# RWKV preparation without Pool: paired low-rank halves and attention keys loaded in quarters in an encoder block on one core

## The chip, the core and the metric

The kernel runs on one core of a Trainium2 chip. A core has five engines that run side by side, each working through its own queue in order: PE (matrix products; PEld is its weight load), DVE (vector operations), ACT (scalar functions, with a table of functions that is loaded when another set is needed), POOL (a general vector engine) and SP, which here only issues DMAs. POOL and ACT issue DMAs too. PE writes into PSUM, DVE and ACT read PSUM; POOL reads the on-chip memory SBUF only. Semaphores order the engines among each other. The metric is device time in microseconds (us) from the start to the end of one execution; lower is better.

## The reference

One layer of a bidirectional encoder: one input projection feeds windowed attention, a two-directional RWKV-7 scan and sigmoid gates; then output projection, MLP and a gated input embedding. Sequence 1024, width 1024, 8 RWKV heads of 64. What the changed stage prepares is the RWKV part:

```python
h = rms_norm(x, norm_mix[i])
proj = h @ w_in[i]
...
zr = proj[..., O_RWKV:O_GATE]
zr = zr + shift_mu[i] * (centred_shift(zr) - zr)      # 0.5 * (previous + next token)
...
w_raw = w0 + einsum('btr,drc->dbtc', tanh(wl), w2)    # wl, al: 64 columns of zr each
decay = exp(-exp(-softplus(-w_raw) - 0.5))
a = sigmoid(a0 + einsum('btr,drc->dbtc', al, a2))
kk = k * k_k
kk = kk / maximum(sqrt(sum(kk * kk, axis=-1)), 1e-12)
k_dir = k * (1.0 + (a - 1.0) * k_a)
ys = rwkv7_bidir_scan(r, decay, k_dir, v, -kk, kk * a)
...
bonus = einsum('bthn,dbthn,dhn->bth', r, k_dir, r_k) * v
...
gates = sigmoid(proj[..., O_GATE:])
```

## The kernel before

Activations stand with channels on the 128 rows and tokens along the columns. A product in float32 is made of three matmuls on rounded parts: `split` (L186) rounds a tile to its high part on ACT and subtracts it for the low part on DVE, or on the engine given as `lo_eng`. `load_w` brings a 1024 x 128 block of weights in two DMAs of 256 KB, each with a `split` whose low half is POOL's unless it says otherwise. A projection of 128 channels is 2 halves of 512 tokens x 8 blocks x 3 = 48 matmuls (`proj_steps`, `proj_with`).

The preparation goes over four pairs of heads p. For each pair:

- `keys(p)` projects and mixes the key (`shifted`, L532), squares it into `nrm[:, 0]` (L644) and splits the square; `sums2` (L593, L594) sums it over each head's channels on PE.
- `normed_keys` projects the receptance r; behind its 38th matmul (RH = 36) the sums are put on PE and clamped by DVE (L655). ACT then takes logarithm and exponential (L658, L659, a table load each), DVE makes kk (L661).
- `direction(d, p, ...)` for d = 0, then, after the value projection, for d = 1. `lora` makes two low-rank products (i = 0 the decay `th`, i = 1 the in-context rate `ta`): per half of the tokens a product over all 128 rows (L569) that carries high x high and low x high together, and one over 64 rows (L571). Two full ones, two half-row ones, then the same for the other i. Then scaling on ACT (L670), a running sum on DVE (`TENSOR_TENSOR_SCAN`, L672, with the constant `scan`), E and Ei = exp of plus and minus the sum on ACT (L682, L683), the operands ra and bk (L687, L688 on POOL, L695, L696), kd (L691, L692) and rk for the bonus (L698 to L701). ra and bk go to DRAM.
- `add_bonus` of a pair runs during the next pair: rk split and summed on PE, the value turned by PE transposes (L607), product bv on DVE (L612).

`shifted` copies the projection to zr on ACT (L539) and writes it scaled by 1 - mu (L542); POOL adds the two neighbours (sm, L544), DVE multiplies by mu/2 and adds (L545).

In the last pair, `fill0` draws steps from `gates0`, the sigmoid gates' projection of the first token half (24 matmuls a gate; F0 tells how many steps where). What is left of `gates0` runs at low priority among the attention's matmuls. After pair 2, one POOL DMA of 2 MB loads the attention's keys kT (L727) into the room of `nrm` (tag `yk`). Attention starts with the queries' DMA, also on POOL (L879), and its scores `sc` (L894).

What order the instructions of an engine take is decided by a scheduler from the order of the code, priorities and dependencies; an operation may be pinned with `keep_in_program_order` (`mmo` is a pinned matmul). Tiles of one tag share `bufs` buffers, and a new tile waits until the old one in its buffer is done with.

Of the kernel before, what the change touches and what calls it, by code (L numbers as in the profile page):

```python
# [9 lines left out]
F32 = mybir.dt.float32  # L10
F32R = mybir.dt.float32r
# [30 lines left out]
RH = 36  # L42
# [11 lines left out]
F0 = (28, 28, 28, 28, 40)  # L54
# [84 lines left out]
def block_kernel(ctx: ExitStack, tc: tile.TileContext, I: dict, out: bass.AP):  # L139
# [45 lines left out]

    def split(hi, lo, src, lo_eng=None, pin=False):  # L186

        a = nc.scalar.copy(hi, src)  # L188
        b = (lo_eng or nc.vector).tensor_tensor(out=lo, in0=src, in1=hi.bitcast(F32), op=ALU.subtract)  # L189
        if pin:  # L190
            tc.keep_in_program_order(a)
            tc.keep_in_program_order(b)
# [111 lines left out]
    def gates(h, ms=range(2 * KT), mm=nc.tensor.matmul):  # L304

        for m in ms:
            c0 = O_GATE + m * P
            hi, lo = load_w(PW, "w", w_in[:, :, c0:c0 + P], P, parts=2)
# [189 lines left out]
    with ExitStack() as s1:  # L498
# [15 lines left out]
        nc.vector.memset(wsc, W_SCALE)  # L514
        hka = A1.tile([P, 4], F32, name="hka")
# [7 lines left out]
        for i in range(2):  # L523
            st = A1.tile([P, ND, 512], F32, name="wlrst", tag="th", bufs=2)
# [4 lines left out]
        scan = A1.tile([P, T], F32, name="scan")  # L529
        nc.sync.dma_start(scan, I["scan"])  # L530

        def shifted(c0, mi, pss=None, pin=False):  # L532
            pss = pss or proj(c0)
            zr = A1.tile([P, T + 2], F32, name="zr", bufs=1)
            nc.vector.memset(zr[:, 0:1], 0.0)
            nc.vector.memset(zr[:, T + 1:T + 2], 0.0)
            zc = z = A1.tile([P, T], F32, name="z", bufs=4)
            for h in range(2):
                a = nc.scalar.copy(zr[:, 1 + 512 * h:513 + 512 * h], pss[h])  # L539
                if pin and h == 0:  # L540
                    tc.keep_in_program_order(a)
                nc.scalar.activation(out=zc[:, 512 * h:512 * h + 512], in_=pss[h], func=AF.Copy, scale=omm[:, mi:mi + 1])  # L542
            sm = A1.tile([P, T], F32, name="sm", bufs=1)
            nc.gpsimd.tensor_tensor(out=sm, in0=zr[:, 0:T], in1=zr[:, 2:T + 2], op=ALU.add)  # L544
            a = nc.vector.scalar_tensor_tensor(out=z, in0=sm, scalar=hmu[:, mi:mi + 1], in1=zc, op0=ALU.mult, op1=ALU.add)  # L545
            if pin:
                tc.keep_in_program_order(a)
# [10 lines left out]
        sg = A1.tile([P, T], F32, name="sg", tag="th", bufs=2)  # L558
# [4 lines left out]
        def lora(d, p, i, bias_col):  # L563

            th = A1.tile([P, T], F32, name="th", bufs=2)
            cs_, hss = slice(p * P, (p + 1) * P), [slice(512 * h, 512 * h + 512) for h in range(2)]
            pss = [PX.tile([P, 512], F32, name="px", tag="px", bufs=6) for _ in range(2)]
            for ps, hs in zip(pss, hss):
                nc.tensor.matmul(ps, wlr_h[i][:, d, cs_], lr[i][:, hs], start=True, stop=False)  # L569
            for ps, hs in zip(pss, hss):  # L570
                nc.tensor.matmul(ps, wlr_l[hrows[i], d, cs_], lr[i][hrows[i], hs], start=False, stop=True)  # L571
            for h, ps in enumerate(pss):
                nc.scalar.activation(out=th[:, 512 * h:512 * h + 512], in_=ps, func=AF.Tanh, scale=0.5, bias=hb[:, bias_col:bias_col + 1])
            return th
# [41 lines left out]
        gates0 = gates(0)  # L616
# [21 lines left out]

        nrm = PY.tile([P, 2, T], F32, name="nrm", tag="yk")

# [8 lines left out]
        def normed_keys(p, kz, sums):  # L649

            ri = nrm[:, 1]

            def norms():
                for hs, ps in next(sums):
                    nc.vector.tensor_scalar_max(ri[:, hs], ps, 1e-24)  # L655
# [6 lines left out]
            return kz, rz, kk  # L662
# [3 lines left out]

# [1218 lines left out]
```

## Time and profile before

| | us |
|---|---|
| three runs, median | 3303.46 |
| lowest and highest of the three | 1796.93, 4185.17 |
| the profiled execution's own time | 1788.35 |
| its span, first to last instruction | 1786.6 |
| preparation, first key matmul to first score | 122.8 to 369.7 |
| mean granted PE clock | 0.98 |

A profile row of the timeline gives start and duration in us, engine, line, operation, output <- inputs, shapes and how often (x); in brackets stands how long the engine was idle before it and what ended that. A row of the waits gives who waited for whom, total us, times, longest. A row of windows gives, for a stretch, its length and each engine's busy us and instructions (x). A row of DMA issues ends with KB each and us from issue to landing.

### The profile page before, as it was taken

The numbers are of one execution on the slowest core, as the hardware profiler recorded it, in microseconds if no ns is written. First come the engines' busy times: TensorE is split into PE (matmuls) and PEld (weight loads), VectorE is DVE, ScalarE is ACT, GpSimd is POOL, SyncE is SP. The second block draws the span as 40 slices with busy tenths as digits, with TensorE's granted clock in tenths as the row PEclk, the third lists the DMA queues.
The fourth block names the chain that finished last, engine by engine and source line by source line (L and its number), as shares of the span: only waits on it lengthen the run. The fifth ranks groups of instructions, "written<-read, shape, count | busy, mean of one in ns | idle before, by whom it ended". The sixth has DMA issues, their size and how long they took to land. (4 is left out here: it accounts for less than half of the span.)

```text
span 1786.6 us, 29998 instructions
## 1 busy us (share of the span) xinstructions
PE 1689.6 (95%) x11544; PEld 1353.2 (76%) x11544; DVE 1148.1 (64%) x1955; ACT 884.8 (50%) x1624; POOL 276.7 (15%) x239
## 2 busy tenths in 40 slices
PE   7999998899999999988899989999999999999998
PEld 7987675666677777766568867888888888888887
DVE  6657887455936565766563487676675877685432
ACT  5547775357755655555531345444444444554221
POOL 3343224422132222121232000000000000000000
PEclk9999999999999999989899989999999999999999
DMA  6353455574355363553564305544547973574111
GB/s 202 93 140 109 144 153 184 167 219 125 95 166 153 98 183 96 153 158 119 185 216 147 118 36 177 166 140 153 165 136 257 312 256 117 185 219 142 52 44 45
DMA packets 272271, 269.20 MB, mean 151 GB/s; under 512 B 47872, under 2 KB 194176, under 8 KB 272000
## 3 DMA queue, kind: packets, MB, share of 16 engines
q1 hardware_dynamic: 263872, 253.98, 45.8%
q0 software_dynamic: 7824, 12.59, 2.5%
q8 instruction: 91, 1.49, 0.4%
q10 hardware_dynamic: 432, 0.73, 0.2%
q14 instruction: 52, 0.43, 0.1%
HBM read 186.49 MB, written 80.74 MB: 150 GB/s over the span
## 5 line engine op out<-in xcount | busy, mean ns | idle before, releaser
L1767 PE MATMUL ff2ps<-tl,sh 128*128 128x512 f32 x448 | 174.5, 389 | 0.0
L1767 PE MATMUL ff2ps<-th,sl 128*128 128x512 f32 x448 | 174.4, 389 | 0.0
L1767 PE MATMUL ff2ps<-th,sh 128*128 128x512 f32 x448 | 173.9, 389 | 0.0
L189 POOL TENSOR_TENSOR wlo<-wst,whi 128x512 fp32r<-128x512 f32 x76 | 103.6, 1378 | 272.9 <-ACT whi L188 268.1
L176 POOL TENSOR_TENSOR rstd<-ms,neghalf 128x1 f32<-128x1 f32 x24 | 13.2, 552 | 792.9 <-DVE ms L174 792.9
L188 ACT CAST sh<-sst 128x512 fp32r<-128x512 f32 x109 | 67.8, 622 | 99.8 <-PE ff2ps L1767 52.9
L189 DVE TENSOR_TENSOR sl<-sst,sh 128x512 fp32r<-128x512 f32 x109 | 75.1, 689 | 48.1 <-ACT sh L188 47.8
L1767 PEld LDWEIGHTS ff2ps<-th,sh 128*128 128x128 f32 x448 | 84.0, 188 | 17.9 <-ACT th L188 0.4
L1767 PEld LDWEIGHTS ff2ps<-tl,sh 128*128 128x128 f32 x448 | 84.1, 188 | 17.9 <-DVE tl L189 0.5
L1767 PEld LDWEIGHTS ff2ps<-th,sl 128*128 128x128 f32 x448 | 84.1, 188 | 17.4
L188 ACT CAST whi<-wst 128x512 fp32r<-128x512 f32 x100 | 60.0, 616 | 53.8 <-DMA wst<-in_w_in_dram 26.0
L188 ACT CAST w1h<-w1st 128x512 fp32r<-128x512 f32 x48 | 28.4, 620 | 105.7 <-DMA w1st<-in_w_ff_dram 66.2
L189 DVE TENSOR_TENSOR w1l<-w1st,w1h 128x512 fp32r<-128x512 f32 x48 | 31.8, 688 | 52.3 <-ACT w1h L188 52.3
L1092 DVE TENSOR_TENSOR gm<-gps,gmask 128x512 f32<-128x512 f32 x64 | 42.2, 683 | 28.9 <-PE gps L209 28.9
L219 PE MATMUL mm<-hh,wlo 128*128 128x512 f32 x144 | 58.2, 404 | 2.5 <-DVE wlo L189 2.5
L219 PE MATMUL gmm<-hh,wlo 128*128 128x512 f32 x144 | 58.8, 408 | 1.2 <-POOL wlo L189 1.1
L215 PE MATMUL mm<-hh,whi 128*128 128x512 f32 x144 | 58.2, 404 | 1.7 <-ACT whi L188 1.7
L215 PE MATMUL gmm<-hh,whi 128*128 128x512 f32 x144 | 58.4, 406 | 1.5 <-ACT whi L188 1.3
L217 PE MATMUL gmm<-hl,whi 128*128 128x512 f32 x144 | 58.3, 405 | 0.0
L217 PE MATMUL mm<-hl,whi 128*128 128x512 f32 x144 | 57.5, 399 | 0.0
L1123 ACT ACTIVATE rac<-rac,Dt 128x128 f32<-128x128 f32 x120 | 40.3, 393 | 27.0 <-PE gps L209 24.9
L189 DVE TENSOR_TENSOR w1l<-ssum,w1h 128x512 fp32r<-128x512 f32 x64 | 43.0, 687 | 16.1 <-ACT w1h L188 16.1
(409 smaller groups left out, 4972.6 us busy)
## 6 DMA issues: line engine op xcount, KB each, us to landing
wst<-in_w_in_dram SPq DMA_DIRECT2D x92, 256.0 KB, 3.5
tst<-in_w_ff_dram SPq DMA_DIRECT2D x80, 256.0 KB, 3.9
w1st<-in_w_ff_dram SPq DMA_DIRECT2D x32, 512.0 KB, 5.3
hid_S<-h SPq DMA_DIRECT2D x64, 256.0 KB, 2.2
sst<-hid_S SPq DMA_DIRECT2D x64, 256.0 KB, 2.8
hid_A<-h SPq DMA_DIRECT2D x48, 256.0 KB, 2.0
sst<-hid_A SPq DMA_DIRECT2D x45, 256.0 KB, 3.9
ra_d<-ra SPq DMA_DIRECT2D x8, 1024.0 KB, 4.9
```

What stands on the lines that cost most here:

```text
L176: nc.gpsimd.tensor_tensor(out=r, in0=ms, in1=neghalf.broadcast_to([P, width]), op=ALU.pow)
L188: a = nc.scalar.copy(hi, src)
L189: b = (lo_eng or nc.vector).tensor_tensor(out=lo, in0=src, in1=hi.bitcast(F32), op=ALU.subtract)
L215: mm(ps, ah, bh, start=(i == 0), stop=False)
L217: mm(ps, ah, bl, start=False, stop=False)
L219: mm(ps, al, bh, start=False, stop=(i == n - 1))
L1092: nc.vector.tensor_tensor(out=gm[d][:, s % NB, q::2, :], in0=pss[q], in1=gmask[:, d, :].unsqueeze(1).broadcast_to([P, NP, P]), op=ALU.mult)
L1123: nc.scalar.activation(out=r_, in_=r_, func=AF.Copy, scale=Dt[:, d, j, s - 1:s])
L1767: nc.tensor.matmul(banks[bs][i], x_[:, isl], y_, start=fresh and p + j == 0, stop=p == NPR - 1 and j == 2, skip_group_check=True)
```

## The change

- `shifted`: ACT's copy to zr is scaled by mu/2 as well, and DVE adds the two neighbours to z in two additions; POOL's addition and its tile are gone; zr has two buffers.
- `low_rank` takes the place of `lora`: both i together, the four full products first, then the four half-row ones with i alternating, all pinned. For direction 0 it is called, with the running sum (`decays`), ahead of the receptance projection.
- The key sums stand behind the whole receptance projection; the clamp is ACT's: max(s, 1e-24) as relu(s - 1e-24) + 1e-24.
- ra's second half goes from POOL to DVE; rk's first product from DVE to ACT.
- The constant `scan` moves into `nrm`. th gets a third buffer.
- Gates 0 to 4 take their low weight halves on DVE. `fill0` draws 56, 56 and four times 12 steps instead of 28 four times and 40.
- kT is loaded behind the last pair in four quarters of 256 tokens, each after the low half last given to POOL, 12 gate steps behind each.
- The first queries' DMA is issued ahead of the other work of attention, and the zeroing of zi moves behind the second block of attention.

```diff
-F0 = (28, 28, 28, 28, 40)
+F0 = (56, 56, 12)
...
-    def gates(h, ms=range(2 * KT), mm=nc.tensor.matmul):
+    def gates(h, ms=range(2 * KT), mm=nc.tensor.matmul, lo_of=lambda m: nc.gpsimd):
...
-        scan = A1.tile([P, T], F32, name="scan")
+        nrm = PY.tile([P, 3, T], F32, name="nrm", tag="yk")
+        scan = nrm[:, 2]
         nc.sync.dma_start(scan, I["scan"])
...
             for h in range(2):
-                a = nc.scalar.copy(zr[:, 1 + 512 * h:513 + 512 * h], pss[h])
...
-            sm = A1.tile([P, T], F32, name="sm", bufs=1)
-            nc.gpsimd.tensor_tensor(out=sm, in0=zr[:, 0:T], in1=zr[:, 2:T + 2], op=ALU.add)
-            a = nc.vector.scalar_tensor_tensor(out=z, in0=sm, scalar=hmu[:, mi:mi + 1], in1=zc, op0=ALU.mult, op1=ALU.add)
...
+                nc.scalar.activation(out=zr[:, 1 + 512 * h:513 + 512 * h], in_=pss[h], func=AF.Copy, scale=hmu[:, mi:mi + 1])
+                nc.scalar.activation(out=z[:, 512 * h:512 * h + 512], in_=pss[h], func=AF.Copy, scale=omm[:, mi:mi + 1])
+            for i in (0, 2):
+                nc.vector.tensor_tensor(out=z, in0=z, in1=zr[:, i:i + T], op=ALU.add)
             return z
...
+        def low_rank(p, d):
...
+            for i in range(2):
+                for ps, hs in zip(pss[i], hss):
+                    mmo(ps, wlr_h[i][:, d, cs_], lr[i][:, hs], start=True, stop=False)
+
+            for h, hs in enumerate(hss):
+                for i in range(2):
+                    mmo(pss[i][h], wlr_l[hrows[i], d, cs_], lr[i][hrows[i], hs], start=False, stop=True)
...
-        gates0 = gates(0)
+        gates0 = gates(0, lo_of=lambda m: nc.vector if m < 5 else nc.gpsimd)
...
-            rz = shifted(O_RWKV + p * P, p, proj_with(O_RWKV + p * P, {RH: norms}))
-            nc.scalar.activation(out=ri, in_=ri, func=AF.Ln)
+            th, ta = low_rank(p, 0)
+            th = decays(0, th)
+            rz = shifted(O_RWKV + p * P, p)
+
+            for hs, ps in next(sums):
+                nc.scalar.activation(out=ri[:, hs], in_=ps, func=AF.Relu, bias=tiny[:, 0:1])
+            nc.scalar.activation(out=ri, in_=ri, func=AF.Ln, bias=tiny[:, 1:2])
...
-            nc.gpsimd.tensor_tensor(out=ra[:, :, 1, :], in0=ch(rz), in1=E2, op=ALU.mult)
-            ta = ta()
+            nc.vector.tensor_tensor(out=ra[:, :, 1, :], in0=ch(rz), in1=E2, op=ALU.mult)
...
-                nc.vector.tensor_scalar_mul(rk, kd, col("r_k", p))
+                nc.scalar.activation(out=rk, in_=kd, func=AF.Copy, scale=col("r_k", p))
...
-            if p == NP - 2:
-                kT = PY.tile([P, 2, 2, T], F32R, name="kT", tag="yk")
-                nc.gpsimd.dma_start(kT, kT_d)
-
-        fill0(NP - 1, 4)
+        kT = PY.tile([P, 2, 2, T], F32R, name="kT", tag="yk")
+        for q in range(4):
+            ts = slice(256 * q, 256 * q + 256)
+            a = nc.gpsimd.dma_start(kT[:, :, :, ts], kT_d[:, :, :, ts])
+            if q:
+                after(a, on_pool[0])
+            fill0(NP - 1, 2)
```

What moves on the engines, at three places. First PE, at the low-rank products of direction 0 of pair 1. Before, behind ten last matmuls of the receptance projection:

```order
L219 MATMUL mm<-hh_90,wlo 128x512
L569 MATMUL px<-lr_1373,wlrh_1358 128x512 x2
L571 MATMUL px<-lr_1373,wlrl 128x512 x2
L569 MATMUL px<-lr_1374,wlrh_1359 128x512 x2
L571 MATMUL px<-lr_1374,wlrl 128x512 x2
L215 MATMUL mm<-hh_92,whi 128x512
```

The changed kernel has, at a low-rank group:

```order
L223 MATMUL mm<-hh_90,wlo 128x512
L213 MATMUL px<-lr_1376,wlrh_1361 128x512 x2
L213 MATMUL px<-lr_1377,wlrh_1362 128x512 x2
L213 MATMUL px<-lr_1376,wlrl 128x512
L213 MATMUL px<-lr_1377,wlrl 128x512
L213 MATMUL px<-lr_1376,wlrl 128x512
L213 MATMUL px<-lr_1377,wlrl 128x512
L231 MATMUL mm<-hh_92,whi 128x512
```

The full products stand together, and neighbours among the half-row ones (wlrl) take different halves of the rows; each full and half group is entered once instead of twice. Second DVE, from the running sum of direction 0 of a middle pair on. Before (s and s2l are the low parts of a split, nrm the clamped key sums):

```order
L672 SCALAR_TENSOR_TENSOR th<-scan,th 128x1024
L692 TENSOR_TENSOR kd<-kd,z 128x1024
L684 COPY Dt<-E 128x16
L687 SCALAR_TENSOR_TENSOR ra<-kk,E 128x16x64
L693 SCALAR_TENSOR_TENSOR th<-th,kk 128x1024
L696 TENSOR_TENSOR bk<-kd,Ei 128x16x64
L695 SCALAR_TENSOR_TENSOR bk<-th,Ei 128x16x64
L698 TENSOR_SCALAR rk<-kd,pc 128x1024
```

In the changed kernel:

```order
L682 SCALAR_TENSOR_TENSOR th<-nrm,th 128x1024
L191 TENSOR_TENSOR s_1407<-nrm,s_1407 128x512
L191 TENSOR_TENSOR s2l<-nrm,s2h 128x512
L715 TENSOR_TENSOR rk<-rk,z 128x1024
L692 MEMSET E 128x16
L699 COPY Dt<-E 128x16
L544 MEMSET zr 128x1
L545 MEMSET zr 128x1
L706 TENSOR_TENSOR kd<-kd,z 128x1024
L191 TENSOR_TENSOR wlo<-wst,whi 128x512 x2
L710 TENSOR_TENSOR bk<-kd,Ei 128x16x64
```

The running sum has moved ahead of the split of the key's square, and the memset that E waits for now comes behind it, behind the split and behind a product of the pair before. Third POOL, from the third pair's end to the first queries. Before:

```order
L544 TENSOR_TENSOR sm<-zr 128x1024
L727 DMA kT<-kT_d 128x4096
L189 TENSOR_TENSOR wlo<-wst,whi 128x512 x2
L688 TENSOR_TENSOR ra<-z,E 128x16x64
L189 TENSOR_TENSOR wlo<-wst,whi 128x512 x2
L688 TENSOR_TENSOR ra<-z,E 128x16x64
L189 TENSOR_TENSOR wlo<-wst,whi 128x512
L544 TENSOR_TENSOR sm<-zr 128x1024
L189 TENSOR_TENSOR wlo<-wst,whi 128x512 x11
L745 MEMSET zi 32x32x32
L746 MEMSET zi 32x32x32
L879 DMA qT<-qT_d 128x1024 x2
```

In the changed kernel:

```order
L740 DMA kT<-kT_d 128x4x256
L191 TENSOR_TENSOR wlo<-wst,whi 128x512 x2
L740 DMA kT<-kT_d 128x4x256 x2
L191 TENSOR_TENSOR wlo<-wst,whi 128x512 x2
L740 DMA kT<-kT_d 128x4x256
L191 TENSOR_TENSOR wlo<-wst,whi 128x512 x4
L882 DMA qT<-qT_d 128x1024 x2
L759 MEMSET zi 32x32x32
```

The first quarter is POOL's first work since the splits ahead of the first pair, gate 5's low halves stand right behind it, and the queries' DMAs have passed the memsets of zi.

More of the change, by code (lines that the diff above doesn't have):

```diff
@@ L41 @@
 VH = 8
-RH = 36
 TPAT = (1, 3)
@@ L514, in block_kernel @@
         nc.vector.memset(wsc, W_SCALE)
+        tiny = A1.tile([P, 2], F32, name="tiny")
+        nc.vector.memset(tiny[:, 0:1], -1e-24)
+        nc.vector.memset(tiny[:, 1:2], 1e-24)
         hka = A1.tile([P, 4], F32, name="hka")
@@ L865, in ps_att, with queries @@
             return PA.tile(shape, F32, name=name, tag="tp", bufs=3)
+        def queries(n):
+            qT = A2.tile([P, NH, P], F32R, name="qT", bufs=2)
+            nc.gpsimd.dma_start(qT, qT_d[n])
+            return qT
+        qT0 = queries(0)
         low0 = low_products(BI, ps_att, 0, nc.tensor.matmul)
@@ L877, in block_kernel @@
         for n in range(NT):
-            qT = A3.tile([P, NH, P], F32R, name="qT", bufs=2)
-            nc.gpsimd.dma_start(qT, qT_d[n])
+            qT = queries(n) if n else qT0
             k0, k1 = max(n - 1, 0), min(n + 2, NT)
```

72 lines of the change are left out of this document (34 added, 38 removed).

## The prediction

> **What bounds the kernel now.** I read the page first: its engine shares say who could be the limit.
>
> ```profile
> span 1786.6 us, 29998 instructions
> ...
> PE 1689.6 (95%) x11544; PEld 1353.2 (76%) x11544; DVE 1148.1 (64%) x1955; ACT 884.8 (50%) x1624; POOL 276.7 (15%) x239
> ```
>
> PE is the limit over the whole span, so the change can win only where PE stands or where it has fewer matmuls. The change lies in the RWKV preparation. I cut that stage at PE's channel-sum matmuls of the four pairs' key norms (142.7, 186.3, 233, 279.8) and end it at the first attention score (369.7). Columns: length; busy us (instructions) of PE, PEld, DVE, ACT and POOL; granted clock, DMA share, GB/s.
>
> ```profile
> 122.80:142.70 19.90, 19.90 (x88) 16.18 (x87) 15.36 (x20) 11.44 (x18) 4.34 (x2) 1.00 0.35 102
> 142.70:186.30 43.60, 39.56 (x166) 30.01 (x164) 36.51 (x38) 28.60 (x40) 12.41 (x5) 1.00 0.45 133
> 186.30:233.00 46.70, 43.78 (x178) 33.05 (x179) 41.06 (x45) 32.37 (x47) 11.32 (x5) 0.96 0.49 147
> 233.00:279.80 46.80, 41.27 (x176) 31.31 (x176) 40.28 (x41) 30.94 (x45) 17.59 (x7) 0.99 0.49 147
> 279.80:369.70 89.90, 80.49 (x317) 59.66 (x317) 45.57 (x38) 42.91 (x65) 37.06 (x27) 0.95 0.58 182
> ```
>
> The stage takes 246.9 us. The first row has no hole: 88 matmuls in 19.90 us, 0.226 each; where PE runs on I take 0.23. The later rows hold far fewer matmuls per us. Next, the waits in 122 to 370 us (total, times, longest):
>
> ```profile
> DVE z L545 <- POOL sm L544: 24.0, 6, 12.1
> ...
> ACT nrm L644 <- DVE z L545: 16.5, 3, 8.6
> ...
> PE px L593 <- ACT s L188: 12.0, 3, 5.5
> ...
> ACT E L682 <- DVE E L680: 5.2, 4, 1.7
> ```
>
> The first three are one chain: PE's key sums wait for ACT's square, ACT for DVE's mixed key z, and DVE is late. Why it is late, the timeline at the end of the third period tells:
>
> ```profile
> 263.86 3.12 POOL L688 TENSOR_TENSOR ra<-z,E 128x1024 f32<-128x1024 f32 x1 [7.60 <-ACT E L682]
> ...
> 264.83 2.18 DVE L684 COPY Dt<-E 128x16 f32<-128x16 f32 x1
> ...
> 269.26 2.87 POOL L544 TENSOR_TENSOR sm<-zr 128x1024 f32<-128x1024 f32 x1
> ...
> 270.30 2.91 DVE L696 TENSOR_TENSOR bk<-kd,Ei 128x1024 f32<-128x1024 f32 x1
> ...
> 279.78 0.80 PE L593 MATMUL px<-s,one_r 128*128 128x512 f32 x1 [5.54 <-ACT s L188]
> ...
> 282.38 0.63 PE L215 MATMUL mm<-hh,whi 128*128 128x512 f32 x1
> ```
>
> A copy of 16 columns took 2.18 us, until POOL's ra ended at 266.98: beside POOL, DVE stands. PE stands 5.54 us behind that, and its matmuls then last 0.63 and follow each other by 0.43 us (282.38 to 282.81) for some ten of them.
>
> **PE's floor, before.** Ahead of the first score stand 12 projections of 48 matmuls, 214 gate matmuls and 32 channel sums: 822 x 0.23 = 189.1. The low-rank groups, and a group of transposes:
>
> ```profile
> 236.10 0.63 PE L569 MATMUL px<-lr,wlrh 128*128 128x512 f32 x2
> 236.65 0.73 PE L571 MATMUL px<-lr,wlrl 64*128 64x512 f32 x2
> 237.31 0.73 PE L569 MATMUL px<-lr,wlrh 128*128 128x512 f32 x2
> 237.97 0.73 PE L571 MATMUL px<-lr,wlrl 64*128 64x512 f32 x2
> 238.63 0.50 PE L215 MATMUL mm<-hh,whi 128*128 128x512 f32 x1
> ...
> 294.62 1.09 PE L607 MATMUL vtp<-ident,z 128*128 128x128 f32 x8
> ```
>
> One direction of one pair is 238.63 - 236.10 = 2.53 us, eight are 20.2; four groups of eight transposes, overlapping their neighbours, are about 1.0 each, 4.0. Floor 213.3, so 246.9 - 213.3 = 33.6 us are lost: 4 to 6 in each of the three middle windows, and 17 in the last (89.9 less 272 matmuls, 12 sums, two low-rank groups and two groups of transposes, 72.3).
>
> **Low-rank halves side by side.** The high products and the half-row products now stand as two blocks of four, and the halves alternate between rows 0-63 and 64-127. A full product costs about 0.28 (0.55 for two), a half 0.33. If a pair of halves overlaps: 4 x 0.27 + 2 x 0.33 = 1.75, 0.8 less per direction, 6.2 in all. If it doesn't: 4 x 0.27 + 4 x 0.33 = 2.4, 1.1 in all. The nearest row is the attention stage's low products, which alternate between the halves of the rows too:
>
> ```profile
> 425.94 0.27 PE L771 MATMUL lps<-la,lb 64*64 64x64 f32 x1
> ...
> 426.39 0.22 PE L771 MATMUL lps<-la,lb 64*64 64x64 f32 x2
> ```
>
> These are the first and last rows of 26 matmuls of 0.22 or more that start within 0.45 us, so they overlap. I take 6.2. With 211 gate matmuls ahead of the score (0.7 less) the new floor is 206.4.
>
> **DVE per pair.** Prices where POOL is idle:
>
> ```profile
> 165.63 0.74 DVE L698 TENSOR_SCALAR rk<-kd,pc 128x1024 f32<-128x1024 f32 x1
> ...
> 212.49 1.28 DVE L189 TENSOR_TENSOR wlo<-wst,whi 128x512 fp32r<-128x512 f32 x2
> ...
> 214.90 2.28 DVE L672 TENSOR_TENSOR_SCAN th<-scan,th 128x1024 f32<-128x1024 f32 x1
> ...
> 228.98 1.27 DVE L545 SCALAR_TENSOR_TENSOR z<-sm,hmu,z 128x1024 f32<-128x1024 f32 x1
> ...
> 230.18 1.21 DVE L701 TENSOR_TENSOR rk<-rk,z 128x1024 f32<-128x1024 f32 x1
> ...
> 233.41 1.29 DVE L655 TENSOR_SCALAR nrm<-px 128x512 f32<-128x512 f32 x2
> ```
>
> Before, a full pair has 2 scans (4.6), 3 z (3.8), 13 other passes of 1024 columns at 1.21 to 1.28 (15.9), 3 weight splits (3.8), splits of the two sums (2.8), bv (1.3), the clamp (1.3), rk's first product (0.7), small ones (0.7): 34.9. The window 186.30:233.00 shows 41.06 busy; the 6.2 between is the standing beside POOL. After, each z is two additions, 2.42 for 1.27: +3.5 for three; ra's second half comes over from POOL: +2.4; clamp and rk's product go to ACT: -2.0. That is 38.8 with nothing on POOL to stand beside, so DVE gets 2.3 us shorter per pair although it does more. ACT's prices:
>
> ```profile
> 209.09 2.42 ACT L573 ACTIVATE th<-px,hb 128x512 f32<-128x512 f32 x4
> ...
> 230.29 1.15 ACT L644 ACTIVATE nrm<-z,pc 128x1024 f32<-128x1024 f32 x1 [7.39 <-DVE z L545]
> ...
> 232.52 0.58 ACT L539 COPY zr<-mm 128x512 f32<-128x512 f32 x1
> 232.99 0.69 ACT L542 ACTIVATE z<-mm,omm 128x512 f32<-128x512 f32 x1
> ```
>
> ACT gets rk (1.15) and two clamps (1.2), and its plain copies become scaled ones (0.69 for 0.58, six a pair): its 32.37 of a period become 35.4, below PE and DVE.
>
> **Waits that stay.** At direction 0 DVE now does scan, two splits, a product and only then the memset of E; ACT's E waits for that memset (5.2 us over four such waits before), then E, Ei and kd follow, three passes or 3.4 us, which DVE fills only in part with the copy of Dt: I count 2.8 of DVE standing. So a full period is 38.8 + 2.8 = 41.6 by DVE, and 41.0 - 1.6 = 39.4 by PE: 2.2 lost at best. At worst DVE's idle time of now stays, 46.7 - 41.06 = 5.6, period 44.4, 5.0 lost. I take 2.8 for each of the two full periods and 1.4 for the first, which has no bonus: 7 in all. The sums now come after all 48 receptance matmuls and a low-rank group, not after 38: 4 us more room for the chain above, which is why I lean to the lower end; the freed time reaches PE only as far as the sums were late.
>
> **The last stretch, 17 us lost before.** The gates are drawn 56 before the value projection, 56 behind it and 12 with each key quarter, and gates 0 to 4 get their low halves on DVE (5 x 1.28 = 6.4 us there). Walking DVE's new order against PE's by the prices above, the second half of gate 1 waits about 2 us behind pair 3's exponentials, the second half of the value weights 1, the bonus sums 1. At worst the waits for weights of now stay:
>
> ```profile
> 309.41 0.50 PE L215 MATMUL mm<-hh,whi 128*128 128x512 f32 x1 [1.71 <-ACT whi L188]
> ...
> 316.16 0.50 PE L219 MATMUL mm<-hh,wlo 128*128 128x512 f32 x1 [1.42 <-DVE wlo L189]
> ```
>
> I take 9 (between 4 and 14): weights come from DRAM two buffers ahead, and both splits queue behind the pair's own work on ACT and DVE.
>
> **Keys and queries.** Before, the keys' load went out long before use; the queries came last:
>
> ```profile
> 291.61 0.62 POOL L727 DMA_DIRECT2D kT<-kT_d  x1 [2.81 <-DVE zr L536]
> ...
> kT<-kT_d POOLq DMA_DIRECT2D x1, 2048.0 KB, 8.1
> ...
> 369.68 0.59 PE L894 MATMUL sc<-kT,qT 128*128 128x256 f32 x3 [1.29 <-DMA qT<-qT_d]
> ```
>
> Now the scan's constant lies in the tile whose room the keys take, so the first quarter waits on POOL for the last scan, and the low half of gate 5 is queued behind it. From PE's last low-rank group to the first score stand 140 gate matmuls, transposes and sums: 34 us. The last scan ends some 8 us into that (four tanh 2.4, scaling 1.15, three short operations on ACT 1.8, scan 2.3). The issue takes 0.62 and half a gate's split about 1.3 on POOL, which makes 9.9; gate 5's is needed after 50 matmuls, at 11.5. Spare: 1.5 us there, and for the quarters some 15 even at the 8.1 us which all four took as one. I count nothing, and nothing for the wait for queries (at most -1.3); their load is now issued ahead of the zeroing of zi, which runs under attention.
>
> [...]
>
> **Sum.** Stage after: 206.4 + 7 + 9 = 222.4, against 246.9: -24.5. Attention keeps three more gate matmuls, +0.7, and may lose a little to zi: +0.5. So -23.3 against the profiled execution's 1788.35 us (1.75 of it outside the span): 1765. The three runs shown have a median of 3303.46 and a lowest of 1796.93. The profiled execution is 0.5% under that lowest; nothing in its trace could explain the other two, and my number is for executions like it.
>
> **Rivals.**
> - Small gain: DVE keeps its 5.6 us of idle per period and the last stretch loses 14 or more. Stage 206.4 + 13 + 14 = 233.4, -13.5, and 1.2 back: 1776, with more lost behind it up to 1786. For it: ACT at 35.4 and DVE at 38.8 of a 40 us period, each in order, leave little room for one to wait for the other.
> - To the floor: losses of only 5 in all, 211.4: -35.5 and 1.2 back, 1754 (1749 to 1756). For it: the freed 4 us before the sums. Against it: E's wait.
> - The low-rank edit doesn't do what it says, its halves follow each other: 1.1 instead of 6.2, 1770; the row above speaks against it.
> - Slower: the last scan is late, so the first key quarter holds POOL, gate 5 behind it holds PE, and each us beyond the 1.5 spare goes onto the end. It outweighs the gain from 25 us on (28 us late: 1792). Against it: DVE is idle for 44 of the last window's 89.9 us.
>
> **Numbers.** Forecast 1765 (1757 to 1772) 0.50; small gain 0.22; floor 0.13; no overlap 0.08; slower 0.07. The range of 1750 to 1786 leaves out the slower case, a third of the floor's and some of the small gain's upper edge, about 0.15. A measurement of this kernel tells about 2% (36 us) from no change. Faster by that needs under 1752.6, half of the floor's 0.13 and some of its edge: 0.09. Slower by that, over 1824, needs 60 us of late scan: 0.03. Within: 0.88.
>
> **What would show it.** Right: no POOL rows from 122 us to the first key quarter; key sums less than 2 us late in each pair; sums-to-sums periods of 41 to 43 us; DVE copies of Dt at 0.17; half products starting in pairs; a first score near 345. Wrong: periods at 45 (ACT or E's chain binds), PE waiting for wlo of gates 1, 2 or 5 for more than 5 us, key quarters landing after the last gate matmul, or attention longer by what preparation gave.

## The result, and the profile after

| | before | after |
|---|---|---|
| median of five runs, us | 1796.93 | 1781.8 |
| lowest and highest, us | 1788.39, 4185.17 | 1778.6, 1782.72 |
| profiled execution's own time, us | 1788.35 | 1781.66 |
| first attention score, us | 369.7 | 351.5 |
| first uaps matmul (a mark inside the scan), us | 751.6 | 744.7 |

The two long runs of before (3303.46 and 4185.17 us), for which no trace shows a cause, are left out of every comparison here. After takes 0.9939 of before's time (95% interval 0.9911 to 0.9967), 11 us less and within 2%. The forecast was 1765 us, 23 less than before's profiled execution; the two profiled executions differ by 6.7 us.

The page of after has the same engine as the limit; POOL has 62 us less work than before, VectorE ten:

```profile
span 1779.9 us, 29948 instructions
...
PE 1686.6 (95%) x11544; PEld 1356.6 (76%) x11544; DVE 1137.7 (64%) x1977; ACT 895.9 (50%) x1636; POOL 214.3 (12%) x210
```

The windows of the preparation in after, cut at the key sums (now 148.6, 186.4, 226.4, 266.6) and the first score; columns as in the prediction (length, busy us and instructions of PE, PEld, DVE, ACT, POOL, granted clock, DMA share, GB/s):

```profile
122.80:148.60 25.80, 25.80 (x113) 20.52 (x112) 19.26 (x28) 17.40 (x26) 0.00 (x0) 1.00 0.20 63
148.60:186.40 37.80, 37.80 (x166) 29.77 (x165) 34.07 (x41) 32.64 (x46) 0.00 (x0) 1.00 0.54 153
186.40:226.40 40.00, 40.00 (x177) 31.23 (x176) 36.51 (x45) 34.45 (x49) 0.00 (x0) 1.00 0.59 171
226.40:266.60 40.20, 40.15 (x178) 31.26 (x177) 38.28 (x47) 34.41 (x50) 0.00 (x0) 1.00 0.58 171
266.60:351.50 84.90, 72.12 (x296) 55.71 (x295) 38.89 (x39) 36.73 (x57) 19.42 (x17) 0.92 0.64 189
```

Up to the last key sums PE has no hole left: 143.75 of 143.8 us. All that is lost lies in the last row: 12.8 us of idle PE and a clock of 0.92. Behind the first score the gain shrinks. The windows of attention, of the work from the last score to the first qps matmul (the chunk inverses' second step), and on to uaps, for before and then for after:

```profile
369.70:485.30 115.60, 108.99 (x643) 71.09 (x644) 81.14 (x284) 84.06 (x230) 21.24 (x21) 1.00 0.48 134
485.30:515.30 30.00, 28.81 (x149) 20.64 (x147) 17.51 (x42) 17.05 (x34) 14.91 (x15) 1.00 0.65 187
515.30:751.60 236.30, 222.07 (x3901) 179.50 (x3900) 142.86 (x278) 134.01 (x279) 47.29 (x54) 0.98 0.47 132
```

```profile
351.50:467.90 116.40, 107.99 (x632) 70.70 (x631) 84.72 (x284) 84.29 (x230) 21.57 (x21) 0.99 0.48 134
467.90:504.70 36.80, 31.97 (x167) 23.24 (x165) 19.75 (x44) 17.41 (x36) 14.93 (x15) 1.00 0.55 167
504.70:744.70 240.00, 225.59 (x3901) 182.60 (x3901) 141.64 (x274) 134.38 (x279) 47.43 (x53) 0.96 0.45 127
```

From the last score to qps it takes 36.8 us instead of 30.0, with 18 matmuls more and 4.8 us of idle PE instead of 1.2. From there to uaps stand the same 3901 matmuls, 3.7 us longer at a clock of 0.96 instead of 0.98; in a repetition of after (run after_again) that window takes 235.7 us at 0.98, so these 3.7 us are the clock's and not the change's. Such windows give an account of a run from 122.8 us to uaps: idle is the length less PE's busy time, lost clock is the length times one less the granted clock (two decimals, so good to about 1 us a window), and the rest is PE's work. Each row is one profile, and before has only one. The rows below the third are runs of the next section.

| us | length | idle: prep., attention, to qps, to uaps | lost clock | rest |
|---|---|---|---|---|
| before | 628.8 | 21.9, 6.6, 1.2, 14.2 = 43.9 | 12 | 573 |
| after | 621.9 | 12.8, 8.4, 4.8, 14.4 = 40.4 | 18 | 564 |
| after, run again | 618.9 | 13.1, 9.1, 4.9, 14.0 = 41.1 | 11 | 567 |
| kt_mid_split | 610.2 | 9.9, 8.0, 3.7, 13.9 = 35.5 | 10 | 564 |
| zi_first | 612.9 | 15.2, 4.5, 2.8, 14.1 = 36.6 | 14 | 562 |
| fill14 | 610.9 | 17.2, 6.5, 0.0, 13.5 = 37.2 | 15 | 558 |
| lo_dve | 612.1 | 12.0, 5.7, 4.2, 13.7 = 35.6 | 10 | 566 |
| mid_zi | 603.4 | 11.2, 4.7, 1.3, 13.9 = 31.1 | 7 | 565 |

The change took 9 us of idle out of the preparation and put 6 back behind it (22.0 before, 27.6 and 28.0 after), and PE's work fell by 6 to 9. Where the last stretch stands shows in the waits of PE from 122.8 to 351.5 us in after, and in rows of its timeline:

```profile
PE px L604 <- ACT s2h L190: 8.5, 1, 8.5
PE mm L219 <- ACT whi L190: 2.3, 1, 2.3
PE gmm L219 <- ACT gth L316: 1.2, 1, 1.2
PE gmm L223 <- DVE wlo L191: 0.7, 1, 0.7
```

```profile
312.91 0.79 POOL L740 DMA_DIRECT2D kT<-kT_d  x1 [193.73 <-DVE th L682]
...
319.43 1.54 POOL L740 DMA_DIRECT2D kT<-kT_d  x2
...
325.02 0.78 POOL L740 DMA_DIRECT2D kT<-kT_d  x1
...
321.72 2.75 SPq L717 DMA_DIRECT2D bk_d<-bk  x1
324.56 6.08 SPq L317 DMA_DIRECT2D g_d<-gth  x2
...
335.92 0.62 ACT L190 CAST s2h<-rk 128x512 fp32r<-128x512 f32 x1 [8.61 <-DMA g_d<-gth]
...
336.59 0.80 PE L604 MATMUL px<-s2h,one_r 128*128 128x512 f32 x1 [8.49 <-ACT s2h L190]
```

The second half of the bonus split takes a buffer of the gates' tanh tiles (tag `gth`, two buffers) and waits until a tanh store has landed. That store goes out behind 2 MB of ra and bk and beside 2 MB of keys; from 325 to 340 us the DMA share is 1.02. PE idles 8.5 us, and then its next matmuls start 0.43 us apart (338.03 to 338.46, at a granted clock of 0.50) instead of 0.23.

### The profile page after: what moved, and what is told of

Read it like the earlier page. It is cut to its first block, busy times and chain, and to the rows that moved or that the text cites. A ratio compares the mean times of both kernels' runs of the same rounds, so it can differ in the third digit from the quotient of the medians.

```text
span 1779.9 us, 29948 instructions
## 1 busy us (share of the span) xinstructions
PE 1686.6 (95%) x11544; PEld 1356.6 (76%) x11544; DVE 1137.7 (64%) x1977; ACT 895.9 (50%) x1636; POOL 214.3 (12%) x210
## 5 line engine op out<-in xcount | busy, mean ns | idle before, releaser
L191 POOL TENSOR_TENSOR wlo<-wst,whi 128x512 fp32r<-128x512 f32 x66 | 88.5, 1353 | 260.8 <-ACT whi L190 255.4
L1162 DVE COPY Wt<-wps 64x512 f32<-64x512 f32 x16 | 10.9, 680 | 66.0 <-PE wps L213 54.1
L807 DVE TENSOR_TENSOR tmp<-Lp,Z 128x31 f32<-128x31 f32 (+15 forms) x124 | 50.7, 409 | 2.3
L1537 PE MATMUL ff1ps<-fh,w1l 128*128 128x512 f32 x128 | 51.1, 399 | 0.6 <-DVE w1l L191 0.6
```

Of the source, the lines that this page charges most:

```text
L807: nc.vector.tensor_tensor(out=tv, in0=Lp[:, t + 1:32, t:t + 1].broadcast_to([P, n, m]), in1=Z[:, t:t + 1, 0:m].broadcast_to([P, n, m]), op ...
L1537: nc.tensor.matmul(ps, x_[:, k, :], y_[:, k, :], start=start and k + i == 0, stop=k == 3 and i == 2, skip_group_check=True)
```

## The experiments

All are the changed kernel with the edits named. First score and uaps are from one profile each; the ratio is to runs of the kernel before made beside it, with its 95% interval. Every ratio is within 2% of 1. The theories are named by the letters that the expectations give them.

| run | first score | uaps | median us | ratio |
|---|---|---|---|---|
| after_again | 351.5 | 741.7 | 1781.07 | 0.994 (0.9916 to 0.9965) |
| own_split | 348.6 | 743.1 | 1783.08 | 0.996 (0.9946 to 0.9974) |
| kt_early | 349.2 | 743.2 | 1778.63 | 0.9939 (0.9917 to 0.9961) |
| kt_early_split | 350.0 | 744.1 | 1778.92 | 0.993 (0.9906 to 0.9955) |
| kt_mid_split | 347.6 | 733.0 | 1773.75 | 0.9914 (0.9882 to 0.9945) |
| kt_mid_split_gpool | 352.1 | 731.1 | 1774.81 | 0.9902 (0.9876 to 0.9928) |
| serial | 352.2 | 745.7 | 1781.26 | 0.9952 (0.993 to 0.9973) |
| apart | 354.3 | 741.4 | 1784.85 | 0.9979 (0.9965 to 0.9993) |
| shift_pool | 357.6 | 740.8 | 1786.42 | 0.9976 (0.9957 to 0.9995) |
| pool_both | 363.9 | 748.0 | 1790.99 | 1.0005 (0.9994 to 1.0015) |
| zi_first | 353.9 | 735.7 | 1772.39 | 0.9903 (0.9887 to 0.9919) |
| fill14 | 355.6 | 733.7 | 1773.01 | 0.9905 (0.988 to 0.9929) |
| lo_dve | 347.3 | 734.9 | 1772.57 | 0.989 (0.9866 to 0.9914) |
| best | 352.0 | 736.1 | 1775.42 | 0.9921 (0.9909 to 0.9934) |
| best_zi | 352.8 | 733.9 | 1771.21 | 0.9892 (0.9872 to 0.9911) |
| mid_zi | 347.5 | 726.2 | 1765.14 | 0.9855 (0.9835 to 0.9875) |

### The wait in the last stretch

**own_split**

```diff
-        def sums2(w, src):
+        def sums2(w, src, own=False):
...
-                if h:
+                if h and own:
+                    s2b = A1.tile([P, 2, 512], F32R, name="s2b", tag="E", bufs=1)
+                    hi, lo = s2b[:, 0], s2b[:, 1]
+                elif h:
...
-            sums = sums2(one_r, rk)
+            sums = sums2(one_r, rk, p == NP - 1)
```

> The changed kernel with one edit: the second half of the last pair's bonus split gets a buffer of its own (the one that E leaves free) instead of one of the two buffers of the gates' tanh tiles. Theory A (the shared buffer): TensorE's wait of 8.5 us for that split at 328 to 336.6 us is all due to the buffer, so it goes; the first attention score comes at 343 (351.5 in the changed kernel), and the span falls by 6 to 9 us, to 1771 to 1774. Theory B (crowded transfers): the stores and the four quarters of the keys between 313 and 336 us are what is late, and without the buffer the same transfers hold the next thing (gate weights, the first attention operands); the first score comes at 347 or later and the span is 1776 or more. Theory C (what is won ahead of the attention does not reach the end): first score at 343, span still 1776 to 1781.

The split waits no more, but the weights of a gate do: on SP their load stands behind the same two stores and needs 7 us to land. PE waits 7.7 us for them, until 334.80. The buffer is where the wait showed, not what it costs; theory A fell, and the first score (348.6) and the span (1783.0) lie where theory B put them.

```profile
320.89 6.20 SPq L317 DMA_DIRECT2D g_d<-gth  x2
327.19 1.92 SPq L207 DMA_DIRECT2D wst<-in_w_in_dram  x2
...
334.13 1.37 ACT L190 CAST whi<-wst 128x512 fp32r<-128x512 f32 x2 [8.80 <-DMA wst<-in_w_in_dram]
```

**kt_early, kt_early_split**

```diff
+            if p == NP - 2:
+                scans[0] = A1.tile([P, T], F32, name="scan3", tag="z", bufs=4)
+                nc.sync.dma_start(scans[0], I["scan"])
+                kT = PY.tile([P, 2, 2, T], F32R, name="kT", tag="yk")
+                nc.gpsimd.dma_start(kT, kT_d)
...
-            a = nc.gpsimd.dma_start(kT[:, :, :, ts], kT_d[:, :, :, ts])
```

> The changed kernel with the keys loaded in one transfer behind pair 2, as in the kernel before, and a second copy of the scan's mask for the last pair in a free buffer of the shifted projections, so that the keys' buffer is free by then. The bonus split still shares the tanh buffers. Theory A (the shared buffer): the tanh store still lands behind the 2 MB of operand stores, so 3 to 6 us of the wait stay, first score at 346 to 349. Theory B (crowded transfers): without 2 MB of keys between 313 and 333 us the store lands in about 3 us, the wait is under 2 us, first score at 342 to 345. Theory C: whatever the first score, the span is 1776 to 1781.

> Both edits together: keys loaded early in one transfer, and a buffer of its own for the last bonus split. Theories A and B both expect the 8.5 us wait gone and the first score at 341 to 344; A expects it no earlier than with the buffer alone, B expects 3 us or more earlier than with the buffer alone. If what is won passes on, the span is 1769 to 1773; by theory C it is 1776 to 1781.

The late wait fell to 3.8 us (theory A had 3 to 6, B under 2), or to 3.0 for a gate weight with both edits. But the keys, issued at 274.7 and 275.6 us, now ran beside pair 3's first ra and bk, and there PE waited 7.3 and 8.3 us for a gate's tanh on ACT, at some 279 to 289 us. ACT itself stood 8.98 and 9.93 us for a gate's weights (`wst`). The first scores came at 349.2 and 350.0, later than either theory had them (342 to 349 and 341 to 344): the crowd moved with the keys. The spans, 1780.5 and 1778.3, are those of theory C.

> The changed kernel again, beside the three others on one chip. All theories expect the same profile as before it: first score at 351 to 352, the wait of about 8.5 us for the bonus split, span within 3 us of 1779.9; the clock records show where the granted clock falls below 0.9 and whether it does so at the same places.

The first score is at 351.5 again, and the waits are within 0.3 us of after's. But the span is 1772.5, against 1779.9 (see the last section).

**kt_mid_split** (as its text says, without the split's own buffer)

```diff
+            if p == NP - 2:
+                mark = A1.tile([P, 1], F32, name="mark")
+                b = nc.gpsimd.tensor_copy(mark, bv[:, T - 1:T])
+                kTs.append(PY.tile([P, 2, 2, T], F32R, name="kT", tag="yk"))
+                after(nc.gpsimd.dma_start(kTs[0], kT_d), b)
...
-            a = nc.gpsimd.dma_start(kT[:, :, :, ts], kT_d[:, :, :, ts])
```

> The changed kernel with the keys loaded in one transfer behind the end of pair 2's bonus (about 296 us, where the transfers were busy 0.40 of the time), the mask for the last scan in a second buffer; the last bonus split shares the tanh buffers as in the changed kernel. Theory B (crowded transfers): with the keys out of the way of the operand stores at 263 to 286 and at 313 to 336 us, the tanh store lands sooner: TensorE's waits between 266 and 350 us, 12.7 in the changed kernel, fall to 4 to 7 us, and the first score comes at 343 to 346. Theory D (the order of the queues): a gate weight's load stands on SP behind the tanh store, that behind the tanh on ScalarE, and that behind the bonus split, which waits for rk on VectorE at 327 to 329 us; then the transfers matter little, 9 us or more of waits stay, and the first score stays at 348 to 351.

The keys go out at 293.83, beside little else, and land in 8.3 us. The tanh store then lands 5 us earlier:

```profile
293.83 0.56 POOL L631 DMA_DIRECT2D kT<-kT_d  x1 [0.41 <-issue]
...
330.54 0.62 ACT L190 CAST s2h<-rk 128x512 fp32r<-128x512 f32 x1 [4.12 <-DMA g_d<-gth]
```

PE's waits up to the first scores fall from 12.7 to 8.3 us, plus 1.2 for the queries; first score 347.6. That is half-way, and both theories' first scores were missed (343 to 346, 348 to 351): B accounts for the 4 us that went, and D was left for those that stayed (the store still stands on SP behind bk, and bk behind VectorE). The span, 1770.6, is under what theory C allowed, 1776 to 1781.

**kt_mid_split_gpool** adds the own buffer and `(nc.sync if h else nc.gpsimd).dma_start(g_d...)`.

> The keys behind the end of pair 2's bonus, a buffer of its own for the last bonus split, and the tanh stores of the first 16 gates issued by POOL in place of SP, so that no weight's load stands behind a tanh store. Theory D (order of the queues): the waits of TensorE between 266 and 350 us fall to 0 to 3 us, first score at 340 to 343. Theory B (crowded transfers): the bytes are the same, 4 to 7 us of waits stay as with the keys' move alone, first score at 343 to 346. Theory C (what is won ahead of the attention does not reach the end): span 1775 to 1781 in either case.

D's promise failed too: 9.8 us of waits stay, the longest for weights, a gate's (4.3) and a projection's (3.6), and PE stands another 3.3 us right at the first scores, at 352.1. By elimination the total transfers of the stretch, not one queue's order, remain; no run shows that by itself.

### The middle of the preparation

**serial** swaps the two loops of the four half-row matmuls (the edit shown); **apart** puts each product's half rows right behind its whole rows:

```diff
-            for h, hs in enumerate(hss):
-                for i in range(2):
+            for i in range(2):
+                for h, hs in enumerate(hss):
```

> The changed kernel with the low parts of the two low-rank products one behind the other (decay, decay, rate, rate) in place of alternating halves of the rows. If TensorE is the limit up to the sums of the last keys, as its 143.75 busy of 143.8 us says, each group is longer by two matmuls of 0.39 us: 7 groups, +5.6 us, the sums of the last keys at 271 to 273 (266.6 in the changed kernel), periods 41 to 42 us (40.0). The rival: the time is hidden by another engine's chain, sums at 266 to 268. At the end of the span, if all of it passes on, +4 to 7 us.

> The changed kernel with the four low-rank products of a direction in the order of the kernel before: decay whole rows, decay half rows, rate whole rows, rate half rows. With the halves only in another order among the four (run serial) nothing moved: four half-row matmuls took 0.66 us either way. Theory G (the grouping is the gain): the group of eight goes from 1.69 us back to 2 x 1.27 = 2.54 us, as in the kernel before, +0.85 a group; from the first to the last sums of the keys (118.0 us in the changed kernel, 6 groups) 123.1 us, first score at 357 to 358. The rival: the time is hidden, 118 to 119 us, first score at 351 to 352.

From the first to the last key sums it takes 118.0 us in after, 118.3 in serial and 122.3 in apart (0.7 a group; expected 123.1). The first score of apart is at 354.3 (357 to 358 expected), and in time it is 0.4% slower than after, with intervals that just touch. So the gain is real and is the grouping; which half stands where inside the four makes no difference. The 5.6 us expected of serial did not come, and not because another engine hid them: the group itself did not get longer. The timeline of after, serial and apart, at one group each:

```profile
135.72 1.09 PE L213 MATMUL px<-lr,wlrh 128*128 128x512 f32 x4
136.74 0.73 PE L213 MATMUL px<-lr,wlrl 64*128 64x512 f32 x4
137.41 0.51 PE L231 MATMUL mm<-hh,whi 128*128 128x512 f32 x1
```

```profile
137.31 0.73 PE L213 MATMUL px<-lr,wlrl 64*128 64x512 f32 x4
137.97 0.51 PE L231 MATMUL mm<-hh,whi 128*128 128x512 f32 x1
```

```profile
134.96 0.73 PE L213 MATMUL px<-lr,wlrh 128*128 128x512 f32 x2
135.62 0.73 PE L213 MATMUL px<-lr,wlrl 64*128 64x512 f32 x2
136.28 0.50 PE L231 MATMUL mm<-hh,whi 128*128 128x512 f32 x1
```

Four half-row products take 0.66 us, as long as two alone.

**shift_pool** (`(nc.gpsimd if i else nc.vector).tensor_tensor` in `shifted`) and **pool_both** (ra's second half on POOL as well):

> The changed kernel with the second addition of every shifted projection on POOL in place of VectorE (14 additions of 128x1024). If POOL holds the chain, as read from the kernel before, the periods between the sums of the keys rise from 40.0 to 42 to 46 us, TensorE waits again in front of them, and the sums of the last keys come at 273 to 285. The rival: VectorE loses 1.2 us of work a projection, TensorE stays the limit, and the sums of the last keys stay at 266 to 268.

> The changed kernel with the second addition of every shifted projection and the second half of ra on POOL. From the first to the last sums of the keys it is 118.0 us in the changed kernel, 123.7 with the addition alone on POOL, 137.1 in the kernel before, of which the low-rank products make some 5. Theory P (POOL in the chain is the rest): 128 to 133 us with both. The rival: the order of the work (norms, decays and low-rank products earlier) is most of the rest, 123 to 127 us. First score 1 to 1 later by what the sums are later.

From the first to the last key sums it takes 123.7 and 128.8 us, and the first scores are at 357.6 and 363.9. The last sums of shift_pool come at 270.2, between the two ranges expected of it; pool_both is as theory P said (128 to 133). With both, the time is that of before, 1.0005. By these runs POOL in this chain was worth 11 of the 19 us by which before's 137.1 was longer, and the grouping 4. The 4 left fall to the new order of the rest, which no run tests alone; and POOL's addition in these two runs is not the same one as before's.

### Behind the first score

**zi_first** makes zi ahead of attention; **fill14** sets `F0 = (56, 56, 14)`; **lo_dve** gives all weights' low parts of the first 16 gates to VectorE.

> The changed kernel with zi made ahead of the attention, as in the kernel before, which leaves 77 gate matmuls between the last score and the first chunk product in TensorE's order (86 in the changed kernel, 75 in the kernel before) and puts 7 more ahead of the first score. Theory O (the gate matmuls behind the last score are what the attention's gain went to): from the last score to the first chunk product 28.5 to 31.1 us in the runs with 86, 23.5 to 24.3 in those with 75; with 77 it is 24 to 26, first score at 352 to 354, first chunk product at 494 to 496 (496.4 to 497.7). The rival (VectorE's inverse, which ends when it ends, sets the first chunk product): 28 to 31 us and 497 or later.

> The changed kernel with 14 in place of 12 steps of the gates behind each quarter of the keys, zi left where the change put it: 224 gate matmuls stand ahead of the first score in TensorE's order (211), 143 inside the attention (135) and 65 behind the last score (86). Theory O (what the change lost behind the first score is the order of the gate matmuls, 11 more of them behind the last score than before): first score about 3 us later, at 354 to 355, first chunk product at 490 to 493 (496.4 and 497.7), time 4 to 9 us under the changed kernel's, ratio to the kernel before 0.989 to 0.992. The rival Z (it is zi's place itself): first chunk product at 496 or later, ratio 0.993 to 0.996.

> The changed kernel with the low parts of all the weights of the first 16 gates made on VectorE (POOL made those from the sixth gate on). In the changed kernel VectorE's scaling of a masked tile of 128x256, 0.34 us elsewhere, took 3.15 us at 476 us while POOL made two low parts, and TensorE waited 3.1 us for it. Theory S (VectorE is held while POOL works): no such scaling over 1 us between 351 and 500 us, and that wait of TensorE goes. The order moves too: 196 gate matmuls ahead of the first score, 146 inside the attention, 90 behind the last score. Theory O (order of the gates): first score 3 us earlier, at 348, first chunk product no earlier than 496, ratio 0.993 to 0.997. If the held VectorE is the larger cost: first chunk product at 491 to 494, ratio 0.989 to 0.992.

POOL zeroes zi at 347 us in after and at 345 in zi_first: the place of the two memsets hardly moved, yet the time fell by 0.4%. fill14 leaves zi and does the same, so rival Z fell. Theory O's times were missed: the first chunk product came at 490.0 in zi_first (expected 494 to 496), at 495.3 in fill14 (490 to 493), and at 490.8 in lo_dve (no earlier than 496) with 90 gate matmuls behind the last score, the most of all. Its count does show in one stretch. From the last score to the first chunk product it takes 19.6 us with 65 gate matmuls there (fill14), 23.5 with 75 (before), 24.4 and 24.5 with 77 (zi_first, mid_zi), 27.0 with 90 (lo_dve), and 28.5 and 30.3 with 86 (after and its repetition). Theory S held: no scaling takes more than 0.42 us in lo_dve, and PE's wait for it went. In after VectorE's scaling stood until POOL had ended two low parts and two memsets:

```profile
476.07 3.15 DVE L930 TENSOR_SCALAR smk<-smk,es 128x256 f32<-128x256 f32 x1
...
474.71 2.58 POOL L191 TENSOR_TENSOR wlo<-wst,whi 128x512 fp32r<-128x512 f32 x2 [7.20 <-ACT whi L190]
477.23 1.84 POOL L1097 MEMSET Sb<- 128x1024 f32 x2
```

Two of PE's waits stand out between the first score and qps in after. With them stand VectorE's wait for the attention's sinks in after and, in the last row, in before:

```profile
PE pt L933 <- DVE smk L930: 5.8, 5, 3.1
PE sc L912 <- DVE mx L913: 3.3, 2, 2.9
...
354.91 0.17 DVE L895 TENSOR_SCALAR nsink<-sink 128x8 f32<-128x8 f32 x1 [12.66 <-DMA sink<-in_qkn_dram]
```

```profile
365.11 0.17 DVE L876 TENSOR_SCALAR nsink<-sink 128x8 f32<-128x8 f32 x1 [3.67 <-DMA sink<-in_qkn_dram]
```

The wait for the scaling is not new: in before PE waited 6.1 us for it. The wait at the scores is (0.2 us in before). VectorE stands until 354.91 for a small load, issued by ACT at 347.6, that in before was there 4.6 us ahead of the first score. zi_first, fill14 and mid_zi keep 0.3 to 0.7 us of this wait, but in them PE stands 2.6 to 4.1 us for the queries just ahead of the first score; lo_dve keeps 2.7.

Three unlike edits each come out 0.35 to 0.5% under after, with intervals that overlap after's at the edge, and by the account each removes 3 to 6 us of idle PE behind 122.8 us. They share another order of the gate matmuls, and no single wait explains all three; how the gain splits among the waits stays open.

### Together

> A combination: keys loaded behind the end of pair 2's bonus, own buffer for the last bonus split, tanh stores of the first 16 gates by POOL, and the sinks of the attention loaded with the small constants at the start of the preparation (TensorE waited 3.3 us at the first scores for VectorE, which stood at nsink for that load). Expected against the run without the last edit: the 3.3 us wait goes, first chunk product at 487 to 491 (490.9), span 1763 to 1770, ratio to the kernel before 0.986 to 0.992. Theory C (gains ahead of the attention do not reach the end): no better than 0.990.

> The changed kernel with two edits: the keys loaded behind the end of pair 2's bonus and zi made ahead of the attention (77 gate matmuls behind the last score). Alone they gave 0.9914 and 0.9903 of the kernel before, the changed kernel 0.994. If they act at different places, the ahead-of-attention waits and the order behind it, they add: first score at 349 to 351, first chunk product at 485 to 488, ratio 0.985 to 0.988. The rival (both shorten the same chain): first chunk product at 489 to 492, ratio 0.989 to 0.992.

> All edits together: keys behind the end of pair 2's bonus, own buffer for the last bonus split, tanh stores of the first 16 gates by POOL, sinks loaded early, zi ahead of the attention (220, 143 and 69 gate matmuls ahead of the first score, inside, and behind the last). Against the run with the two edits alone it has 8 gate matmuls fewer behind the last score: by theory O first chunk product 1 to 3 us earlier, at 483 to 487, ratio 0.983 to 0.988. The rival (the tanh stores on POOL hold VectorE and the keys' queue): no better than with two edits, 0.988 to 0.992.

mid_zi, the keys in the quiet gap and zi ahead of attention, is the fastest: 0.9855 of before, with its whole interval under after's. It adds as its theory said (first chunk product 485.1, ratio 0.985 to 0.988 expected), with a first score even earlier than expected (347.5 instead of 349 to 351). Its windows, to be set against after's:

```profile
347.50:460.60 113.10, 108.41 (x632) 70.52 (x633) 79.79 (x281) 83.06 (x228) 20.32 (x20) 0.98 0.46 129
460.60:491.60 31.00, 29.70 (x156) 21.58 (x154) 18.28 (x45) 17.93 (x36) 14.70 (x15) 1.00 0.63 178
491.60:726.20 234.60, 220.66 (x3901) 177.93 (x3900) 141.49 (x274) 133.86 (x279) 47.82 (x54) 0.99 0.46 133
```

best and best_zi missed their ranges: with the tanh stores on POOL, 10.2 us of waits stay ahead of the first score in each, and PE stood 3.3 and 2.7 us more at the first scores although the sinks were there early. More edits did less.

## Why the prediction was half right

The forecast of 23.3 us less came out as 6.7 in the profiled executions. Of the 16.6 between, 6.3 lie ahead of the first score (18.2 won instead of 24.5; the first score at 351.5 instead of near 345), 10.1 between the first score and uaps, and 0.2 behind that.

- **Low-rank halves, 0.8 a direction: right.** 2.53 - 1.69 = 0.84 in the trace, 0.7 by apart. The halves overlap as forecast, but not because they alternate between the rows: serial, where they don't, takes as long.
- **Periods, 7 us of loss: mis-sized.** VectorE came to 36.5 and 38.3 us a period (38.8 said), ACT to 34.4 (35.4). But the 2.8 us of standing behind E's memset never reached PE: periods of 37.8, 40.0 and 40.2 (41 to 43 said), PE's own. The stage up to the last sums lost about 3.5 to the floor (143.8 less 140.3, the floor of 206.4 without the last stretch's 66.1). The lean to the lower end was right and should have gone further: pool_both shows that POOL in the chain was the larger part of the lateness, 11 of 19 us.
- **The last stretch, 9 us (4 to 14): failed.** It lost 18.8 (84.9 less 66.1, the part of the floor that lies there): 12.8 of idle PE, and about the rest is what a clock of 0.92 over the stretch costs. "The bonus sums 1" was the term that was wrong most: 8.5 of waiting, with a granted clock of 0.50 until 341 us behind it. The walk along VectorE and PE left out SP's queue and the bytes.
- **Keys, "I count nothing": failed.** The quarters' spare on POOL held, gate 5 held nothing up, and each issue took 0.74 to 0.80 us (0.62 said). But 2 MB moved from 292 us into the stretch where the last ra and bk go out; that costs 4 us at the first score (kt_mid_split, which loads them at 293.83 in one transfer), and they are part of the 18.8 above.
- **Attention, 0.7 + 0.5: failed, the largest.** From first score to uaps it was 381.9 us before, 393.2 and 390.2 after: 8 to 11 lost, 1.2 said. In both profiles of after 6 us of this are idle PE; the clock's part, 6 us in one and 1.5 in the other, does not repeat. Between the last score and qps lie 6.8 and 8.6 us of the loss. I counted gate matmuls only up to the first score, three of them; but 75 stood behind the last score before and 86 after, and the wait for the sinks at the first scores was not in the sum at all. How much each of the two costs stays open.
- **The rivals.** The small gain's range (1776 to 1786) holds the time, by its last stretch and "more lost behind it"; its other condition, 5.6 us of idle per period, is wrong. The floor's condition was right up to the last sums. POOL's key quarters did not make it slower. That mid_zi reaches the forecast's 1765 confirms nothing: it has two more edits.

## What to carry to other kernels

When a load is moved, add up the bytes of the stretch that it moves into: here the wait showed at whatever buffer or weight came last, and mending that one place moved it on (8.5 us for the bonus split in after, 7.7 us for a gate's weights in own_split). When a stage is made shorter, keep an account of idle and lost clock for the stages behind it too, since background work that the scheduler redistributes can give the gain back (here 18.2 us at the first score were 6.9 at uaps). And small edits of such an order are worth trying one by one: here two that by their ratios gave 0.3 and 0.4%, neither of them wholly clear of after's interval, came to 0.8% together, and five did not.

## What was not expected of the hardware

- Half-row matmuls. In serial two of the same rows stand next to each other in the program, yet the four take 0.66 us (137.31 to 137.97), as in after, where they start in pairs, two at 136.74 and two at 137.07. Their order did not matter, the grouping did.
- The clock came down to 0.50 in dips of 3.4, 6.8, 10.2 or 13.7 us each (before and after, twice what windows of 1 us lose), and a run's share of them is not fixed. After and its repetition, the same program, differ by 7.4 us of span; their mean granted clocks of 0.977 and 0.982 over spans of 1779.9 and 1772.5 us make 41 and 32 us lost to the clock. One such place, first after, then its repetition:

```profile
600.00:605.00 5.00, 5.00 (x104) 3.96 (x105) 0.00 (x0) 2.32 (x5) 2.50 (x2) 0.50 0.19 54
605.00:610.00 5.00, 5.00 (x73) 4.38 (x67) 0.71 (x2) 2.90 (x6) 0.00 (x0) 0.50 0.20 57
```

```profile
600.00:605.00 5.00, 4.55 (x159) 3.79 (x158) 0.56 (x1) 4.25 (x9) 2.49 (x2) 1.00 0.20 57
605.00:610.00 5.00, 5.00 (x58) 3.73 (x56) 2.09 (x4) 2.14 (x6) 0.00 (x0) 1.00 0.20 54
```

In after the clock also falls within the 8.5 us of idle PE in the last stretch of the preparation: it is 1.00 in the windows from 328 to 331 us, 0.61 in the next and 0.50 from 332 on. At the place shown it falls at 597.5 behind only some 1.2 us of idle PE (594.9 to 596.1); between 595 and 600 us PE idles 1.07 us in after, at a clock of 0.75, and 1.16 us in the repetition, at 1.00. Why one run pays for such a gap and another does not, no run here shows. So a few us between two profiles of this kernel say little without the clock beside them.
